# A decoder layer on one core: sixty-four bytes more behind each of the four tiles that hold split weights

## The chip, the cores and the metric

The kernel runs on one NeuronCore of a Trainium2 chip. The metric is device time of one execution, in microseconds, smaller is better. Several executions are timed and the median is given; beside them one execution is recorded instruction by instruction with the hardware profiler, and that record is what is called the profile or the trace here.

A NeuronCore has five instruction streams that run at the same time and wait for one another through semaphores: TensorE (PE, matrix products, with a separate row PEld in the profile for loading the stationary operand), VectorE (DVE), ScalarE (ACT), GpSimd (POOL) and SyncE (SP, which issues the DMA transfers here). Their common working memory is SBUF, 128 partitions side by side; an address below is a byte offset within a partition, the same in all 128.

## The reference, cut to what matters

One decoder layer: three token mixers on one normalised input, gated and merged, then a gated MLP with a short causal convolution. All in float32, 1024 positions, width 1024.

```python
h = _rmsnorm(x, g_mix[l])
(sb_q, sb_k, sb_v, ml_q, ml_k, ml_v, ml_o, ml_i, ml_f, xa_q, gate_pre) = jnp.split(
    h @ w_in[l], offsets, axis=-1)
...
merged = (gates[:, :, 0] * (y_sb @ w_sb_out[l])
          + gates[:, :, 1] * (y_ml @ w_ml_out[l])
          + gates[:, :, 2] * (y_xa @ w_xa_out[l]))
x = x + merged @ w_o[l]

h = _rmsnorm(x, g_ffn[l])
u = _causal_dwconv(h @ w_up[l], ff_conv_w[l], ff_conv_b[l])
u_val, u_gate = jnp.split(u, 2, axis=-1)
x = x + (jax.nn.silu(u_gate) * u_val) @ w_down[l]
```

Most of the arithmetic is in the dense products: the input projection, the three output projections with `w_o`, and the MLP.

## The kernel before, in words

**Split operands.** Each dense product is made in a faster number format (fp32r) from two parts per operand: `split` (L136, L137) writes a high part with ScalarE and the remainder, source minus high part, with VectorE. A product of two split operands is then three matmuls into one accumulator, in `mm3`: high by high (L149), high by low (L150), low by high (L151). Each of them streams 512 columns of one operand (the moving one) past a 128 x 128 block of the other (the stationary one, loaded ahead by PEld). The names in the profile's rows stand in the order output<-moving,stationary.

**Tiles in SBUF.** `T(shape, tag)` takes a tile from a pool; each tag has a ring of a fixed number of buffers, and the pool puts the rings one behind the other in SBUF. A page (`pg`, 16 buffers), `h` (16), `y` (2), `raw` (2), `whi` (2) and `wlo` (2) are all 4096 bytes per partition: 1024 numbers of 4 bytes. `whi` and `wlo` hold the split weights in three ways:

- `wsplit` (L139) takes one `whi` for the high parts and one `wlo` for the low parts of a 1024-number weight block. The matmuls of a product then load their stationary blocks in the order whi, whi, wlo. The projections of the first stage, the branch outputs and `w_o` are made so; `product` in the MLP's last stage splits into the same two tags.
- `qring` (L661), for the products in which `seven` computes a 2 x 2 block product with seven half-sized ones, takes one tile for both parts of half a weight block, by turns from `whi` and `wlo`. All twelve matmuls of such a product load from that one tile. The gates, the mLSTM and cross-attention columns of the input projection and the whole of the MLP's first product are made so.
- `mem_w` (L200) loads raw weights of the memory tokens' keys and values by turns into `raw`, `whi` and `wlo`, in the first 30 us.

In `nat_chunks` the roles are exchanged: the activations are stationary and `whi` and `wlo` are streamed. Half-sized tiles, `hf` (4 buffers of 2048 bytes), take the last, half-sized weight block and activation of each of the seven products of the MLP's last stage: twelve matmuls with both operands in `hf`.

**Where the tiles begin.** The built program places the rings as in this table, which gives the first byte of each buffer and its remainder by 256.

| tag | first bytes | remainder by 256 |
|---|---|---|
| `hf` | 19712, then every 2048 | 0 |
| `pg` | 28608, then every 4096 | 192 |
| `h` | 94144, then every 4096 | 192 |
| `y`, `raw` | 159680, 163776, 167872, 171968 | 192 |
| `whi` | 176064, 180160 | 192, 192 |
| `wlo` | 184256, 188352 | 192, 192 |
| `U` (5 buffers of 4096 or 4104 bytes) | 192448, then every 4128 | 192, 224, 0, 32, 64 |
| `me`, then `mw` or `px` | 213088, 217184 | 96 |

So before the change, apart from `hf`, every operand of the split products begins at the same remainder, and offsets inside a tile are multiples of 512 bytes.

**Order.** Each engine runs its instructions in the order in which the code (with a scheduler's priorities) recorded them; the rings' sizes decide how far a split can run ahead of the matmuls that read it.

Of the kernel before, what the change touches and what calls it, by code (L numbers as in the profile page):

```python
# [18 lines left out]
P = 128  # L19
D = 1024  # L20
S = 1024
# [21 lines left out]
def tile_hybrid_layer(ctx: ExitStack, tc: tile.TileContext, xT, memT, vecs, w_t, w_n, w_kv, w_if,  # L43
# [16 lines left out]
    def nm(s):  # L60
        uid[0] += 1
        return f"{s}_{uid[0]}"

    BUFS = {"h": 16, "pg": 16, "U": 5, "y": 2, "raw": 2, "whi": 2, "wlo": 2, "hf": 4, "me": 2,
            "mw": 4, "sm": 22, "px": 2}
    late = [None]

    def T(shape, tag, dt=F32, bufs=None):
        pool = {"mw": mlp, "mst": mlp, "px": late[0]}.get(tag, sb)
        return pool.tile(shape, dt, tag=tag, name=nm(tag), bufs=bufs or BUFS[tag])  # L70

    def page(tag="pg", dt=F32):
        return T([P, S], tag, dt)

    def half(dt=F32):
        return T([P, HALF], "hf", dt)

    def wide():
        return T([P, S], "U")
# [9 lines left out]
    def bank(tag):  # L89
        if tag in ("pj", "pv"):  # L90
            return ps.tile([P, HALF], F32, tag=tag, name=nm("ps_" + tag), bufs=2)
        if px1 is not None:
            if not spare.get(tag):
                t = two(tag)
                spare[tag] = [t[:, 1], t[:, 0]]
            return spare[tag].pop()
        return psx[0].tile([P, HALF], F32, tag=tag, name=nm("ps_" + tag), bufs=2)
# [4 lines left out]
    def hs(h):  # L102
        return slice(h * HALF, (h + 1) * HALF)
# [166 lines left out]
    def x_stats(xp):  # L270
        acc = []
        for i in range(4):
            sq = wide()
            nc.scalar.activation(sq, xp[i], AF.Square)
            acc.append(sq)
            if i:
                nc.vector.tensor_add(acc[0], acc[0], sq)
        a = acc[0][:, hs(0)]
        nc.vector.tensor_add(a, a, acc[0][:, hs(1)])
        return a  # L280
# [212 lines left out]
    a = x_stats(xp[0])  # L493
# [538 lines left out]
    for i in range(3 * KT):  # L1032
        b, n = i // KT, i % KT
# [5 lines left out]
        for h in (1, 0):  # L1039
            p = bank("pj")  # L1040
# [3 lines left out]
            dst, t = merged[n][:, hs(h)], th[:, hs(h)]  # L1044
# [360 lines left out]
```

## Time and profile before

| | |
|---|---|
| three timed executions | 1683.66, 1684.94, 1685.43 us |
| median | 1684.94 us |
| the profiled execution's own time | 1682.28 us |
| its span, first to last instruction | 1680.5 us |
| outside the span | 1.8 us |
| TensorE's mean granted clock | 0.999 of full |
| busy shares: DVE, ACT, POOL | 71%, 49%, 3% |

The profile's groups of instructions give for each line, engine and pair of tiles a count, the busy time in us, the mean duration of one in ns and the idle time of the engine just before. The duration of a matmul runs from its start to its modelled end, and matmuls overlap in the array, so 0.39 us in a row is not what one costs: the cost of a matmul in a dense stretch is the distance from its start to the next one's start, and that is read from the timeline, which prints start and duration of each. The view of busy times by stretch can be limited to the instructions that touch one tile, and then counts them.

### The profile page before, as it was taken

To read this page: it belongs to the slowest core of one execution; us is meant where nothing else is said; L and a number is where in the kernel's file an instruction comes from. 1 tells how busy PE (TensorE), PEld (TensorE's weight loads), DVE (VectorE), ACT (ScalarE), POOL (GpSimd) and SP (SyncE) were. 2 spreads that over 40 slices of the span, in tenths; PEclk is the share of its full clock that TensorE was granted. 3 is DMA by queue.
4 is the path that set the end of the run, shared out by engine and by line. 5 is a ranking of instruction groups with operands and counts; after the bars stand their busy time and mean duration, and the time that the engine had idled before them with its cause. 6 is when DMAs were issued, how large, how long until landed. Compare 5 with 4: busy or idle time off the path is not lost.

```text
span 1680.5 us, 21066 instructions
## 1 busy us (share of the span) xinstructions
PE 1652.2 (98%) x7927; PEld 1337.1 (80%) x7927; DVE 1193.2 (71%) x1682; ACT 819.1 (49%) x1237; POOL 51.8 (3%) x95
## 2 busy tenths in 40 slices
PE   8999999999999999999999999999999999999999
PEld 4777777787777888777788887688888888788887
DVE  5648777777954766555457648998777887789864
ACT  4547677645544445555312334565555555543431
POOL 1000000010000101000000000000000000000000
PEclk9999999999999999999999999999999999999999
DMA  8421011233334565322755354222222221486141
GB/s 295 147 64 33 26 39 51 98 122 114 124 115 151 189 188 169 133 100 82 264 196 191 112 178 167 82 95 90 99 76 76 75 86 66 163 326 238 33 140 72
DMA packets 96248, 212.68 MB, mean 127 GB/s; under 512 B 12416, under 2 KB 36224, under 8 KB 96148
## 3 DMA queue, kind: packets, MB, share of 16 engines
q1 hardware_dynamic: 96148, 211.35, 36.8%
q8 instruction: 62, 1.02, 0.3%
q14 instruction: 38, 0.31, 0.1%
HBM read 156.71 MB, written 54.61 MB: 126 GB/s over the span
## 4 chain that ended last, share of the span: by engine, by line
PE 90%; DVE 4%; ACT 4%; DMA 1%; issue 1%; SPq 0%; POOLq 0%; ACTq 0%; DVEq 0%
PE ps_pj L150 14%; PE ps_pj L149 14%; PE ps_pj L151 14%; PE ps_pv L151 6%; PE ps_pv L149 6%; PE ps_pv L150 6%; PE ps_tr L149 4%; PE ps_tr L151 4%; PE ps_tr L150 4%; PE ps_z L151 2%; PE ps_z L150 2%; PE ps_z L149 2%; PE ps_tr L434 2%; PE ps_pv L448 1%; PE ps_z L226 1%; PE ps_z L1005 1%
## 5 line engine op out<-in xcount | busy, mean ns | idle before, releaser
L150 PE MATMUL ps_pj<-h,whi 128*128 128x512 f32 x620 | 243.3, 392 | 0.0
L136 ACT ACTIVATE whi<-raw 128x512 fp32r<-128x512 f32 (+1 forms) x112 | 93.6, 835 | 185.7 <-PE ps_pj L150 81.4
L149 PE MATMUL ps_pj<-h,whi 128*128 128x512 f32 x412 | 163.7, 397 | 0.0
L149 PE MATMUL ps_pj<-pg,whi 128*128 128x512 f32 x396 | 155.1, 392 | 0.5 <-ACT U L699 0.5
L151 PE MATMUL ps_pj<-pg,wlo 128*128 128x512 f32 x380 | 148.1, 390 | 0.1
L150 PEld LDWEIGHTS ps_pj<-h,whi 128*128 128x128 f32 x620 | 116.5, 188 | 24.4 <-issue 1.0
L151 PE MATMUL ps_pj<-h,wlo 128*128 128x512 f32 x332 | 130.8, 394 | 0.5 <-DVE wlo L137 0.4
L810 DVE SCALAR_TENSOR_TENSOR y<-U,vec,y 128x1023 f32<-128x1023 f32 x88 | 112.4, 1279 | 7.5 <-ACT y L808 7.5
L422 DVE TENSOR_TENSOR_SCAN U<-U 128x512 f32<-128x512 f32 (+3 forms) x96 | 88.5, 964 | 30.7 <-ACT U L415 29.8
L149 PEld LDWEIGHTS ps_pj<-h,whi 128*128 128x128 f32 x412 | 77.4, 188 | 17.1 <-issue 0.9
L137 DVE TENSOR_TENSOR wlo<-raw,whi 128x1024 fp32r<-128x1024 f32 x54 | 66.0, 1222 | 32.0 <-ACT whi L136 32.0
L149 PEld LDWEIGHTS ps_pj<-pg,whi 128*128 128x128 f32 x396 | 74.5, 188 | 16.8 <-ACT U L699 0.9
L151 PEld LDWEIGHTS ps_pj<-pg,wlo 128*128 128x128 f32 x380 | 71.3, 188 | 15.6 <-DVE wlo L137 0.6
L136 ACT ACTIVATE whi<-pg 128x512 fp32r<-128x512 f32 (+1 forms) x59 | 43.4, 737 | 74.8 <-PE ps_pv L150 20.5
L150 PE MATMUL ps_pj<-pg,whi 128*128 128x512 f32 x188 | 74.8, 398 | 0.0
L151 PEld LDWEIGHTS ps_pj<-h,wlo 128*128 128x128 f32 x332 | 62.3, 188 | 14.7 <-DVE wlo L137 1.4
L150 PE MATMUL ps_pv<-h,whi 128*128 128x512 f32 x164 | 63.8, 389 | 0.0
L137 DVE TENSOR_TENSOR whi<-raw,whi 128x512 fp32r<-128x512 f32 x58 | 39.9, 688 | 32.2 <-ACT whi L136 32.1
L808 ACT ACTIVATE y<-U,vec 128x1024 f32<-128x1024 f32 x44 | 54.6, 1241 | 14.8 <-DVE U L712 14.7
L151 PE MATMUL ps_pj<-h,whi 128*128 128x512 f32 x156 | 60.8, 390 | 0.0
L151 PE MATMUL ps_tr<-pg,wlo 128*128 128x512 f32 x144 | 56.0, 389 | 0.0
L436 ACT ACTIVATE y<-ps_tr 128x1024 f32<-128x1024 f32 (+3 forms) x48 | 39.1, 814 | 31.6 <-PE ps_tr L434 31.2
(427 smaller groups left out, 4258.8 us busy)
## 6 DMA issues: line engine op xcount, KB each, us to landing
raw<-in_w_t_dram SPq DMA_DIRECT2D x29, 512.0 KB, 4.2
gate_d<-U SPq DMA_DIRECT2D x24, 512.0 KB, 3.2
U<-gate_d SPq DMA_DIRECT2D x24, 512.0 KB, 4.0
pg<-in_w_up_dram SPq DMA_DIRECT2D x22, 512.0 KB, 3.6
act_d<-y SPq DMA_DIRECT2D x22, 512.0 KB
pg<-in_w_t_dram SPq DMA_DIRECT2D x21, 512.0 KB, 3.9
raw<-in_w_dn_dram SPq DMA_DIRECT2D x18, 512.0 KB, 3.4
raw<-in_w_o_dram SPq DMA_DIRECT2D x16, 512.0 KB, 3.8
```

Of the source, the lines that this page charges most:

```text
L136: nc.scalar.activation(hi, src, AF.Copy)
L137: (eng or nc.vector).tensor_sub(lo, src, hi.bitcast(F32))
L149: nc.tensor.matmul(out, lh, rh, start=start, stop=False, skip_group_check=more)
L150: nc.tensor.matmul(out, lh, rl, start=False, stop=False, skip_group_check=more)
L151: nc.tensor.matmul(out, ll, rh, start=False, stop=stop, skip_group_check=more)
L226: nc.tensor.matmul(pm[m], mg[k // 4][:, c], w[:, hs(kk)], start=(k == 0), stop=(k == KT - 1))
L422: nc.vector.tensor_tensor_scan(f[:, a, 1:w + 1], f[:, a, 1:w + 1], f[:, a, 1:w + 1], 1.0 if o == 0 else f[:, a, 0:1], op0=ALU.mult, op1=AL ...
L434: nc.tensor.transpose(pt[:, a, ts(j)], g[:, a, ts(j)], ident)
L436: nc.scalar.activation(wt[:, :, :w], pt[:, :, :w], AF.Copy)
L448: nc.tensor.matmul(pv[64 * a:64 * a + 64, ts(rb % 4)], sbv[s // 2][:, s % 2, (2 * p + a) * 64:(2 * p + a + 1) * 64], wt[:, a, ts(j)], star ...
L808: nc.scalar.activation(out, u, AF.Identity, bias=bias, scale=taps[0])
L810: nc.vector.scalar_tensor_tensor(out[:, :S - s], u[:, s:], taps[s], out[:, :S - s], op0=ALU.mult, op1=ALU.add)
```

## The change

`T` gives tiles of the tags `whi` and `wlo` 16 numbers (64 bytes) more per partition than are used, and hands out the first 1024 numbers, shaped as before. Nothing is read from or written to the 64 bytes behind them.

```diff
     def T(shape, tag, dt=F32, bufs=None):
         pool = {"mw": mlp, "mst": mlp, "px": late[0]}.get(tag, sb)
+        if tag in ("whi", "wlo"):
+
+            t = pool.tile([P, S + 16], dt, tag=tag, name=nm(tag), bufs=BUFS[tag])[:, :S]
+            return t if len(shape) == 2 else t.rearrange("p (a b) -> p a b", a=shape[1])
         return pool.tile(shape, dt, tag=tag, name=nm(tag), bufs=bufs or BUFS[tag])
```

The instructions of the built program, their order on each of the five engines and their waits are the same, row for row, before and after; what differs is the addresses. The tiles that move are these:

| tag | first bytes after | later than before by | remainder by 256 after |
|---|---|---|---|
| `whi` | 176064, 180224 | 0, 64 | 192, 0 |
| `wlo` | 184384, 188544 | 128, 192 | 64, 128 |
| `U` | 192704, then every 4128 | 256 | 192, 224, 0, 32, 64, as before |
| `me`, `mw`, `px`, `mst` | 213344 and behind | 256 | as before |

The tensors in the chip's main memory stay where they were.

## The prediction

> **What bounds the kernel now.** I read the busy times and the granted clock first, then the chain that ended last, then what TensorE waited for, then the timeline of TensorE in a dense stretch.
>
> ```profile
> span 1680.5 us, 21066 instructions
> PE 1652.2 (98%) x7927; PEld 1337.1 (80%) x7927; DVE 1193.2 (71%) x1682; ACT 819.1 (49%) x1237; POOL 51.8 (3%) x95
> PEclk9999999999999999999999999999999999999999
> PE 90%; DVE 4%; ACT 4%; DMA 1%; issue 1%; SPq 0%; POOLq 0%; ACTq 0%; DVEq 0%
> PE ps_z L226 <- DMA raw<-in_w_kv_dram: 6.3, 1, 6.3
> PE ps_tr L434 <- DVE U L424: 3.7, 5, 1.6
> ```
>
> TensorE is busy for 98% of the span, at full clock, and makes 90% of the chain. Its two longest waits are 6.3 us for the first weights and 3.7 us in five pieces. So only the pace of the matmuls can move the time by much. That pace, far from any restart, is this (the matmuls in between, of the same three lines, are left out):
>
> ```profile
> 999.65 0.39 PE L149 MATMUL ps_pj<-pg,whi 128*128 128x512 f32 x1
> 999.88 0.39 PE L150 MATMUL ps_pj<-h,whi 128*128 128x512 f32 x1
> 1000.11 0.39 PE L151 MATMUL ps_pj<-pg,wlo 128*128 128x512 f32 x1
> ...
> 1003.50 0.39 PE L151 MATMUL ps_pj<-pg,wlo 128*128 128x512 f32 x1
> ```
>
> From 999.65 to 1003.50 there are 17 steps: 3.85 / 17 = 0.2265 us each. Here pages, `whi` and `wlo` all begin at remainder 192 by 256, and the loads and streams inside them are shifted against each other by multiples of 512 bytes.
>
> How many matmuls does the change touch? The view of busy times limited to one tile counts those that read `whi` (first row) and `wlo` (second row):
>
> ```profile
> 0.00:1681.00 1681.00, 941.26 (x3372) 630.46 (x3372) 194.99 (x224) 173.63 (x224) 1.00 0.37 127
> 0.00:1681.00 1681.00, 749.73 (x2572) 481.64 (x2572) 195.01 (x224) 92.12 (x147) 1.00 0.37 127
> ```
>
> The first two counts are PE and PEld: 3,372 + 2,572 = 5,944 matmuls, three quarters of all 7,927. Each ns on the step of one is 5.9 us of the end. About 0.2% of the time (3.4 us) is what a measurement of this kernel can tell from no change; that is 0.57 ns a matmul.
>
> **The change, part by part.** It adds and removes no instruction, wait or transfer, and moves none past another: the count of each is unchanged, and the sum of those terms is 0. What can change is how long an instruction takes at its new address.
>
> *VectorE and ScalarE.* The trace already has splits between tiles that begin at different remainders: sources `raw` and `pg` at 192 like the target, `hf` at 0, `px` and `me` at 96.
>
> ```profile
> L137 DVE TENSOR_TENSOR whi<-raw,whi 128x512 fp32r<-128x512 f32 x58 | 39.9, 688 | 32.2 <-ACT whi L136 32.1
> L137 DVE TENSOR_TENSOR whi<-hf,whi 128x512 fp32r<-128x512 f32 x21 | 14.5, 691 | 19.8 <-ACT whi L136 19.6
> L137 DVE TENSOR_TENSOR whi<-me,whi 128x512 fp32r<-128x512 f32 x8 | 5.5, 686 | 3.2 <-ACT whi L136 3.2
> L136 ACT ACTIVATE whi<-raw 128x512 fp32r<-128x512 f32 x58 | 36.3, 626 | 34.2 <-PE ps_pv L151 22.3 <-issue 6.1 <-PE ps_tr L151 2.1
> L136 ACT ACTIVATE whi<-hf 128x512 fp32r<-128x512 f32 x21 | 13.1, 624 | 2.4 <-PE ps_pv L151 2.4
> L136 ACT ACTIVATE whi<-me 128x512 fp32r<-128x512 f32 x8 | 5.0, 629 | 3.8 <-PE ps_pv L151 2.5 <-PE ps_z L151 1.3
> ```
>
> Means of 688, 691 and 686 ns on VectorE and 626, 624 and 629 on ScalarE: 5 ns apart at most. For the 448 VectorE instructions on the two tiles that bounds the cost at 2.2 us either way, and it lies under TensorE's 98%; with that cover gone it would still be below what can be told. I take 0. `U`, `me`, `mw` and `px` move by 256 bytes and keep their remainders; I take 0 for them too, with the same 2.2 us as bound.
>
> *Loads into the moved tiles.* The 6.3 us wait at the start ends with a transfer into `raw`, which isn't moved. 0.
>
> *The weight load.* It now starts at remainders 192, 0, 64 or 128. The trace has loads from other remainders: transposes that load from `U` (192, 224, 0, 32, 64), `pg` (192) and `hf` (0), and products whose weights lie in `hf`.
>
> ```profile
> L434 PEld LDWEIGHTS ps_tr<-ident,U 128*128 128x128 f32 x288 | 31.9, 140 | 13.2 <-issue 7.9 <-ACT y L436 2.8 <-ACT pg L136 0.8
> L916 PEld LDWEIGHTS ps_tr<-ident,pg 128*128 128x128 f32 x32 | 4.0, 139 | 1.0
> L247 PEld LDWEIGHTS ps_tr<-ident,hf 128*128 128x128 f32 x8 | 1.0, 140 | 0.3
> L149 PEld LDWEIGHTS ps_pj<-h,whi 128*128 128x128 f32 x412 | 77.4, 188 | 17.1 <-issue 0.9 <-DVE U L1048 0.8 <-ACT h L136 0.2
> L149 PEld LDWEIGHTS ps_pj<-hf,hf 128*128 128x128 f32 x8 | 1.5, 188 | 0.3
> ```
>
> 139 to 140 ns for transposes and 188 for products, wherever the block begins. The load itself costs nothing more or less.
>
> *The pace of load and stream together.* This is the one term that the trace doesn't settle: nowhere does a long run of split products have stationary and moving operand at different remainders. The nearest rows are the twelve matmuls with both operands in `hf`, at remainder 0, after pages at 192:
>
> ```profile
> 1673.62 0.39 PE L151 MATMUL ps_pj<-pg,wlo 128*128 128x512 f32 x1
> 1673.84 0.39 PE L149 MATMUL ps_tr<-hf,hf 128*128 128x512 f32 x1
> ...
> 1674.07 0.39 PE L150 MATMUL ps_tr<-hf,hf 128*128 128x512 f32 x1
> ...
> 1674.73 0.69 DVE L1229 TENSOR_TENSOR U<-U,ps_tr 128x512 f32<-128x512 f32 x1 [9.42 <-PE ps_tr L151]
> ...
> 1676.38 0.39 PE L151 MATMUL ps_pj<-hf,hf 128*128 128x512 f32 x1
> ```
>
> While the matmul at 1673.62 streams from a page, the first block of `hf` is loaded: exactly the mixed case. Its step is 0.22 us, to the last digit that the row has the dense pace. But the eleven steps within `hf` take 2.54 us, 0.2309 each: 4.4 ns over the dense pace, although both operands have equal remainders again. Two readings are possible. Either a jump between remainders disturbs the pace for some ten matmuls, or the end of a product does (VectorE's evictions start in the same stretch, at 1674.73). Upper end: 4.4 ns on all 5,944, 26.2 us. Lower end: the nearest wide matmuls with a shorter regular step, the scores of the cross-attention, plain float32 with 256 columns, where a matmul is two records.
>
> ```profile
> 669.84 1.73 PE ps_z L980 x8
> ```
>
> 1.73 / 8 = 0.2163 us a record, 10.2 ns under the dense pace; on 5,944 that is 60.6 us. So the term lies between -60.6 and +26.2 us. I take the row nearest to the mixed case, the step at 1673.62, and that is 0.
>
> On the pace the Trainium skill, "TensorE: Matmul & The Clock Gate", section "Wait — 56ns, not 53.3ns?", gives 215.7 ns from start to start with 512 columns at full clock; by it the split products would have 10.8 ns to lose, and an estimate from that page is 64 us for 5,944. The trace's 226.5 ns disagrees with the page's figure, in another number format. On whether the address can free it, "SBUF — State Buffer", section "Who interferes with whom", says that TensorE has two separate read ports, for the stream and for the weight load, and waits for no one: by that rule the sum is 0. No row here shows ports; the 0.22 us step of the mixed case agrees with it.
>
> **Sum.** 0 (instructions) + 0 (splits) + 0 (transfers) + 0 (weight load) + 0 (pace) = 0, against the profiled execution's 1682.28 us, of which 1680.5 are span and 1.8 lie around it. That execution lies 2.7 us under the median of the three timed ones, so the median to expect is theirs, 1684.9 us.
>
> **Rivals.**
>
> *Slower: the jump disturbs.* The mechanism is the first reading above. Before, the remainder jumps into and out of `hf` only seven times each. After, each product of `seven` loads from the next of four tiles, so the distance between stationary and moving operand changes every twelve matmuls, and with `wsplit` it changes twice in every three (whi, whi, wlo). If each jump of the stationary operand costs what the passage into `hf` costs, nearly all 5,944 run at 0.2309: +26 us, 1711. If only the products of `seven` settle again or the disturbance is smaller, a third of that: +9, 1694. It decides from 0.57 ns a matmul on. For it: eleven slow steps that no wait explains. Against it: in `hf` the moving operand jumps too, and the pages that are streamed past `whi` and `wlo` don't move here; and the one step in which only the stationary block had jumped was not slow.
>
> *Faster: equal remainders are the reason for the slow pace.* If the stream and the weight load meet in the same part of SBUF because all tiles begin alike, and that is what separates 0.2265 from 0.2163, shifts of 64 to 192 bytes free part or all: three quarters of the loads are shifted, so up to 0.75 x 60.6 = 45 us, 1640; with a tenth of it 4.5 us, 1680. For it: the gap is there, in nearly every step. Against it: the step with mixed remainders should have been shorter and isn't, and shifts by any multiple of 512 bytes, of which the dense stretch has many, all give the same pace.
>
> *It doesn't do what it says.* A pool could round the longer tiles up so that all remainders stay alike; the addresses in the built program exclude it, so this gets no chance.
>
> **How the numbers follow.** No change: 0.62. The jump disturbs, or some other cost of the mixed remainders: 0.23. Shorter steps: 0.15. The unchanged case holds its own range of 1682 to 1688 (the executions before lie between 1683.66 and 1685.43). Of the slower case's 0.23 I put 0.16 below 1702 (two thirds of the full price), of the faster one's 0.15 about 0.06 above 1677, since there a small gain is less likely than the whole. 1677 to 1702 then leaves out 0.07 above and 0.09 below. The ends that the bounds allow, 1640 and 1711, lie outside.
>
> **What would show it.** One group of those that read `whi` stands for the others:
>
> ```profile
> L150 PE MATMUL ps_pj<-h,whi 128*128 128x512 f32 x620 | 243.3, 392 | 0.0
> ```
>
> Right, if in the changed kernel's timeline a dense stretch of L149, L150 and L151 still has steps of 0.2265 us whichever of the four tiles the weights lie in; if that group stays at 392 ns; and if L136 and L137 keep 624 to 629 and 686 to 691 ns. The slower rival would show as steps of 0.23 and matmuls of 0.40 us scattered through products of `seven`, the faster one as steps towards 0.22. The forecast would be wrong if the steps depend on which tile holds the weights; the twelve matmuls of one product against those of the next tell that at once.

## The result, and the profile after

The changed kernel takes 1703.79 us (median of four, 1703.12 to 1706.60) against 1684.30 us for the kernel before (median of four): ratio 1.0121, 95% interval 1.0109 to 1.0133. It is slower by 1.2%, outside the range of the prediction. Its span in the profile is 1702.0 us, 21.5 us more than before. The line numbers are four higher than before: L149 to L151 are now L153 to L155.

The page's busy times and granted clock, and TensorE's longest waits, of the changed kernel:

```profile
span 1702.0 us, 21066 instructions
PE 1674.5 (98%) x7927; PEld 1339.3 (79%) x7927; DVE 1194.9 (70%) x1682; ACT 819.2 (48%) x1237; POOL 52.4 (3%) x95
PEclk9999999999999999999999999999999999999999
PE ps_z L230 <- DMA raw<-in_w_kv_dram: 6.2, 1, 6.2
PE ps_tr L438 <- DVE U L428: 3.6, 5, 1.6
```

TensorE's busy time has grown by 22.3 us, VectorE's by 1.7 and ScalarE's by 0.1. TensorE's carries the whole difference; the clock is full, and the longest waits are within 0.1 us of what they were. The same matmuls, as many as before, follow one another more slowly. The groups that the prediction named, of the changed kernel:

```profile
L154 PE MATMUL ps_pj<-h,whi 128*128 128x512 f32 x620 | 245.3, 396 | 0.0
L153 PEld LDWEIGHTS ps_pj<-h,whi 128*128 128x128 f32 x412 | 77.6, 188 | 18.1 <-DVE U L1052 1.0 <-issue 0.9 <-ACT h L140 0.2
L141 DVE TENSOR_TENSOR whi<-hf,whi 128x512 fp32r<-128x512 f32 x21 | 14.5, 692 | 20.6 <-ACT whi L140 20.4
L140 ACT ACTIVATE whi<-hf 128x512 fp32r<-128x512 f32 x21 | 13.1, 624 | 2.5 <-PE ps_pv L155 2.5
```

Loads (188 ns) and splits (692 and 624 ns) are as before. The matmul group has gone from 392 to 396 ns. The timeline shows where. These are the first matmuls of five products of `seven` in a row; the eleven others of each are left out:

```profile
466.34 0.39 PE L153 MATMUL ps_pj<-pg,whi 128*128 128x512 f32 x1
...
469.09 0.40 PE L153 MATMUL ps_pj<-h,wlo 128*128 128x512 f32 x1
...
471.88 0.39 PE L153 MATMUL ps_pv<-h,whi 128*128 128x512 f32 x1
...
474.68 0.40 PE L153 MATMUL ps_pj<-h,wlo 128*128 128x512 f32 x1
...
477.48 0.39 PE L153 MATMUL ps_pv<-pg,whi 128*128 128x512 f32 x1
```

Twelve steps take 2.75 us in the first product and 2.79, 2.80 and 2.80 in the next three, which is 0.2292 a step against 0.2325 to 0.2333; before, every one had 0.2265. By the program's addresses their weights lie 0, 128, 64 and 192 bytes from the streamed pages, by remainder. So the pace depends on the tile that holds the weights, which is what the prediction had named as the sign that it was wrong. Even the first product, at 0 as before the change, is slower than it was then; what came just before it counts too, as the run history below shows. In what follows, *distance* is the start of the stationary block minus the start of the streamed one, by remainder of 256.

### The profile page after: what moved, and what is told of

Same layout as the page of the kernel before. It is cut to its first block, busy times and chain, and to the rows that moved or that the text cites. A ratio compares the mean times of both kernels' runs of the same rounds, so it can differ in the third digit from the quotient of the medians.

```text
span 1702.0 us, 21066 instructions
## 1 busy us (share of the span) xinstructions
PE 1674.5 (98%) x7927; PEld 1339.3 (79%) x7927; DVE 1194.9 (70%) x1682; ACT 819.2 (48%) x1237; POOL 52.4 (3%) x95
## 4 chain that ended last, share of the span: by engine, by line
PE 90%; ACT 4%; DVE 4%; DMA 2%; issue 1%; POOL 0%; POOLq 0%; SPq 0%; ACTq 0%; DVEq 0%
PE ps_pj L153 14%; PE ps_pj L154 14%; PE ps_pj L155 14%; PE ps_pv L154 6%; PE ps_pv L155 6%; PE ps_pv L153 6%; PE ps_tr L153 4%; PE ps_tr L154 4%; PE ps_tr L155 4%; PE ps_z L155 2%; PE ps_z L154 2%; PE ps_z L153 2%; PE ps_tr L438 1%; PE ps_pv L452 1%; PE ps_z L230 1%; PE ps_z L1009 1%
## 5 line engine op out<-in xcount | busy, mean ns | idle before, releaser
L153 PE MATMUL ps_pj<-h,whi 128*128 128x512 f32 x412 | 165.2, 401 | 0.5 <-DVE U L1052 0.5
L153 PE MATMUL ps_pj<-pg,whi 128*128 128x512 f32 x396 | 157.1, 397 | 0.7 <-ACT U L703 0.4
L155 PE MATMUL ps_pj<-pg,wlo 128*128 128x512 f32 x380 | 150.0, 395 | 0.1
L155 PE MATMUL ps_pj<-h,wlo 128*128 128x512 f32 x332 | 131.9, 397 | 0.5 <-DVE wlo L141 0.4
L153 PEld LDWEIGHTS ps_pj<-h,whi 128*128 128x128 f32 x412 | 77.6, 188 | 18.1 <-DVE U L1052 1.0
L153 PEld LDWEIGHTS ps_pj<-pg,whi 128*128 128x128 f32 x396 | 74.6, 188 | 19.4 <-ACT U L703 1.3
L155 PEld LDWEIGHTS ps_pj<-pg,wlo 128*128 128x128 f32 x380 | 71.5, 188 | 17.4 <-DVE wlo L141 0.6
L140 ACT ACTIVATE whi<-pg 128x512 fp32r<-128x512 f32 (+1 forms) x59 | 43.4, 737 | 80.5 <-PE ps_pv L154 21.5
L155 PEld LDWEIGHTS ps_pj<-h,wlo 128*128 128x128 f32 x332 | 62.5, 188 | 15.9 <-DVE wlo L141 1.4
L141 DVE TENSOR_TENSOR whi<-raw,whi 128x512 fp32r<-128x512 f32 x58 | 39.9, 688 | 33.2 <-ACT whi L140 33.0
L155 PE MATMUL ps_pj<-h,whi 128*128 128x512 f32 x156 | 61.4, 394 | 0.0
L155 PE MATMUL ps_tr<-pg,wlo 128*128 128x512 f32 x144 | 56.9, 395 | 0.0
L141 DVE TENSOR_TENSOR wlo<-raw,wlo 128x512 fp32r<-128x512 f32 x58 | 39.9, 688 | 22.6 <-ACT wlo L140 22.4
```

The costliest lines, as they stand in the source:

```text
L140: nc.scalar.activation(hi, src, AF.Copy)
L141: (eng or nc.vector).tensor_sub(lo, src, hi.bitcast(F32))
L153: nc.tensor.matmul(out, lh, rh, start=start, stop=False, skip_group_check=more)
L155: nc.tensor.matmul(out, ll, rh, start=False, stop=stop, skip_group_check=more)
```

## The experiments

Three theories stood against one another. **A**: the standing distance sets the pace. **B**: only a change of the distance disturbs, for some ten matmuls (the prediction's slower rival). **C**: the remainder of the stationary block alone counts.

### The distance by itself: scan

A kernel with nothing but bursts of 32 fp32r matmuls, 512 columns, TensorE alone. Names give the bytes: m192w64 streams from remainder 192 and loads from 64.

```diff
+PLAN = [(192, w) for w in range(0, 512, 16)] + [(m, w) for m in (0, 64, 128) for w in range(0, 512, 64)]
+    for n, (m, w) in enumerate(PLAN):
+        p = ps.tile([P, HALF], F32, tag="z", name=f"m{m}w{w}z", bufs=2)
+        for i in range(BURST):
+            a = m // 4 + HALF * (i % 2)
+            b = w // 4 + P * (i % 4)
+            nc.tensor.matmul(p, wts[:, b:b + P], mov[:, a:a + HALF], start=(i == 0), stop=(i == BURST - 1))
```

> Leaves the whole layer out: only split-format matmuls (128x512, 32 in a row into one bank) from two tiles, TensorE alone, the stationary block beginning w bytes and the stream m bytes behind a multiple of 512; m192 with w from 0 to 496 in steps of 16, then m 0, 64, 128 with w in steps of 64. Theory A (the standing distance between stream and weight load sets the pace): groups with w = m run at 0.2267 us a matmul, w = m + 64 near 0.2333, m + 128 near 0.232, m + 192 near 0.229, the same in all 32, whatever m is. Theory B (only a change of the distance disturbs, for about ten matmuls): every group starts with steps near 0.231 and then runs at 0.2267, a mean of 0.228, whatever w is. Theory C (the remainder of the stationary block alone counts, 192 good): w = 192 is quick for every m.

The timeline of the scan merges each burst into a row. The distance from one row's start to the next one's, by 32, is the pace:

```profile
83.32 7.63 PE L70 MATMUL m192w160z<-mov,wts 128*128 128x512 f32 x32
90.78 7.43 PE L70 MATMUL m192w176z<-mov,wts 128*128 128x512 f32 x32
98.06 7.42 PE L70 MATMUL m192w192z<-mov,wts 128*128 128x512 f32 x32
105.31 7.42 PE L70 MATMUL m192w208z<-mov,wts 128*128 128x512 f32 x32
112.57 7.62 PE L70 MATMUL m192w224z<-mov,wts 128*128 128x512 f32 x32
120.03 7.63 PE L70 MATMUL m192w240z<-mov,wts 128*128 128x512 f32 x32
...
246.21 7.45 PE L70 MATMUL m0w0z<-mov,wts 128*128 128x512 f32 x32
253.50 7.63 PE L70 MATMUL m0w64z<-mov,wts 128*128 128x512 f32 x32
260.97 7.60 PE L70 MATMUL m0w128z<-mov,wts 128*128 128x512 f32 x32
268.41 7.49 PE L70 MATMUL m0w192z<-mov,wts 128*128 128x512 f32 x32
275.74 7.43 PE L70 MATMUL m0w256z<-mov,wts 128*128 128x512 f32 x32
283.01 7.63 PE L70 MATMUL m0w320z<-mov,wts 128*128 128x512 f32 x32
```

At equal remainders, 98.06 to 105.31 is 7.25 / 32 = 0.2266 us. With the stream at 0, distance 64 gives 0.2334, 128 gives 0.2325, 192 gives 0.2291, and 256 is quick again. B would have a mean of 0.228 in every burst, and the slow bursts have 0.2325 to 0.2334, so B doesn't describe them. C falls too: m0w0 loads from remainder 0 and is quick (0.2278, with the first steps of the burst, which still settle), and m0w192 loads from 192 and has 0.2291. At a stream of 192 the bursts 16 bytes either side (w176, w208) are quick too. One thing didn't fit A: with the stream at 192, the burst at 128, distance 192, took 0.2334 and not 0.229. No burst was quicker than those at equal remainders. The rows are one execution.

### The distance in the layer: shift64, all64, pad256

Unused bytes move whole rings, either all four weight buffers alike (shift64) or the pages with them (all64). In pad256 the change's own padding is four times as long.

```diff
# shift64, against the kernel before; all64 has "pg" in place of "whi"
+        if tag == "whi" and not spaced:
+            spaced.append(sb.tile([P, 16], F32, tag="gap", name="gap"))
+            nc.gpsimd.memset(spaced[0], 0.0)
# pad256, against the changed kernel
-            t = pool.tile([P, S + 16], dt, tag=tag, name=nm(tag), bufs=BUFS[tag])[:, :S]
+            t = pool.tile([P, S + 64], dt, tag=tag, name=nm(tag), bufs=BUFS[tag])[:, :S]
```

> The kernel before with 64 unused bytes once ahead of the first whi buffer, so all four buffers begin 64 bytes later than the pages by remainder, and keep one distance among themselves. Theory A: all 5,944 run at the pace that products with that distance have in the changed kernel, 0.2333 against 0.2267: +39 us, 1723. Theory B: the distance changes as seldom as before, so 1685. Theory C: as A, 1723.

> The kernel before with 64 unused bytes ahead of the pages, so that pages, h, y, raw, whi and wlo all begin at remainder 0 like hf. Theory A: 1684, since all distances are multiples of 512, and the slow steps at hf are gone (0.4 us). Theory B: 1684. Theory C: 1723, since every stationary block begins at remainder 0.

> The changed kernel with 256 bytes in place of 64 behind each of the four tiles: they begin 0, 256, 512 and 768 bytes later, all remainders by 256 as before. If the distance counts by 256 or less (A, C with period 256): 1684. If it counts by 512 (A with period 512): half of the products are at distance 256, and the time lies between 1690 and 1705. Theory B, if a jump by 256 is a jump: 1700.

| | median | ratio to before (95% interval) |
|---|---|---|
| shift64 | 1716.65 us | 1.0193 (1.0177 to 1.0208) |
| all64 | 1684.08 us | 0.9996 (0.9986 to 1.0005) |
| pad256 | 1683.66 us | 1.0000 (0.9990 to 1.0009) |

The kernel before had 1684.46 us beside them. shift64 keeps one standing distance and is slower than the change itself: B gives 1685 for it and falls as the main cause. all64 loads from remainder 0 and is not slow: C falls again. pad256 jumps by 256 bytes as often as the change jumps by 64, and costs nothing: 256 bytes are a full turn. The first matmuls of two products in shift64, and the first and last of the twelve `hf` matmuls in all64:

```profile
1300.03 0.40 PE L153 MATMUL ps_pv<-h,whi 128*128 128x512 f32 x1
...
1302.83 0.40 PE L153 MATMUL ps_tr<-h,wlo 128*128 128x512 f32 x1
```

```profile
1676.36 0.39 PE L153 MATMUL ps_tr<-hf,hf 128*128 128x512 f32 x1
...
1678.85 0.39 PE L155 MATMUL ps_pj<-hf,hf 128*128 128x512 f32 x1
```

In shift64 2.80 / 12 = 0.2333 us, as in the scan at 64. Its 32 us are less than the 39 expected. In the profiles TensorE's busy time is 34.4 us longer than before (1686.6 against 1652.2) and the span 33.2 us (1713.7 against 1680.5), so waits that are now covered make about 1 us of the gap. The 5,944 also count some matmuls in plain float32 and some that stream `whi` or `wlo`; how much that makes was not worked out. In all64 the eleven steps take 2.49 us, 0.2264 each, where the kernel before had 0.2309: with pages and `hf` at one remainder the slow passage is gone. That was the row from which the prediction took its upper end.

### How near is near enough: late16 and late32

```diff
# late16, against the changed kernel; late32 has 8 in place of 4
-            t = pool.tile([P, S + 16], dt, tag=tag, name=nm(tag), bufs=BUFS[tag])[:, :S]
+            t = pool.tile([P, S + 64], dt, tag=tag, name=nm(tag), bufs=BUFS[tag])[:, 4:S + 4]
```

> The changed kernel with the four tiles each beginning 16 bytes later than a page by remainder (256 bytes longer, used from byte 16 on). The scan had 0.2267 us a matmul at distances of 16 either way. Theory A with that window: 1684, within 0.2% of the kernel before. If in the full kernel any unequal remainder is slow: 1717, as in shift64.

> As late16, but 32 bytes later. The scan had 0.2334 us a matmul at a distance of 32 (w224 beside m192), 6.7 ns over the quick pace. Theory A with the scan's window: as shift64, whose 5,944 matmuls ran 6.6 ns slower: 1717, between 1713 and 1720. If the window were wider in the full kernel: 1684.

late32 came out as expected, 1715.81 us, ratio 1.0192 (1.0175 to 1.0209). late16 fits neither expectation: 1705.43 us, ratio 1.0133 (1.0098 to 1.0169), and its four executions scatter from 1699.32 to 1713.04, where those of every other version of the layer lie within 5.3 us. Its timeline, two products at the same distance 16 in one execution:

```profile
466.96 0.39 PE L153 MATMUL ps_pj<-pg,whi 128*128 128x512 f32 x1
...
469.76 0.39 PE L153 MATMUL ps_pj<-h,wlo 128*128 128x512 f32 x1
```

```profile
1300.02 0.39 PE L153 MATMUL ps_pj<-pg,whi 128*128 128x512 f32 x1
...
1302.74 0.39 PE L153 MATMUL ps_z<-h,wlo 128*128 128x512 f32 x1
```

2.80 us for twelve steps in the first, 0.2333 each, and 2.72 in the second, 0.2267. One distance, two paces. So theory A lacked something, and a new one was needed.

### What came before: history

Theory **H**: at some distances two repeating patterns of steps exist, and the state in which a burst begins picks one. Pairs of bursts, the first at one distance and the second at another; d16p64then is distance 16 after 64.

```diff
+PLAN = [x for d in (16, 192, 240, 128, 32, 0) for p in (0, 64, 32, 128) for x in ((p, f'd{d}p{p}first'), (d, f'd{d}p{p}then'))]
```

> Leaves the whole layer out: TensorE alone, fp32r, 512 columns, stream at remainder 0. Pairs of bursts of 32: first at distance 0, 64, 32 or 128, then at the distance d asked for (16, 192, 240, 128, 32, 0). Theory H (a distance can have two standing patterns, and what came before picks one; this is why the layer at distance 16 scattered from 1699 to 1713): d16 after 0 runs at 0.2267 us a matmul, d16 after 64 or 32 near 0.233; d192 near 0.229 after one and 0.233 after another. Theory N (the distance alone decides, and the slow stretches of the layer at 16 come from other engines' work): d16 runs at 0.2267 after every predecessor, and each d has one pace. Both: d0 returns to 0.2267 within ten matmuls.

```profile
15.88 7.42 PE L70 MATMUL d16p0then<-mov,wts 128*128 128x512 f32 x32
...
30.61 7.63 PE L70 MATMUL d16p64then<-mov,wts 128*128 128x512 f32 x32
...
60.44 7.42 PE L70 MATMUL d16p128then<-mov,wts 128*128 128x512 f32 x32
...
74.95 7.49 PE L70 MATMUL d192p0then<-mov,wts 128*128 128x512 f32 x32
...
89.74 7.63 PE L70 MATMUL d192p64then<-mov,wts 128*128 128x512 f32 x32
...
326.44 7.45 PE L70 MATMUL d0p64then<-mov,wts 128*128 128x512 f32 x32
```

Here the second number, first start to last end, is compared: 7.42 us is a burst at about 0.2267 a step, 7.63 one at about 0.2334. Distance 16 is quick after 0 and after 128 and slow after 64 and 32 (7.63 both), with no other engine at work. Distance 192 is 7.49 after 0 and 7.63 after 64, so the burst of the scan that hadn't fitted has the second of two paces (there it came after distance 176). Distance 240 took 7.42 after 0 and 7.47 or 7.48 after the others; 32 and 128 were slow after every predecessor (7.59 to 7.62). Distance 0 comes back to the quick pattern after every predecessor tried. H holds and N falls. It fits the scatter of late16: which pattern a stretch falls into depends on its beginning, and chance delays could throw it from one into the other (this last step was not tried by itself).

The changed kernel shows the same in the layer. In the products of the MLP's first stage the four tiles come in another order than in the five products of the result, where it was 0, 128, 64, 192:

```profile
1142.39 0.39 PE L153 MATMUL ps_pv<-pg,whi 128*128 128x512 f32 x1
...
1145.12 0.39 PE L153 MATMUL ps_tr<-h,wlo 128*128 128x512 f32 x1
...
1147.87 0.40 PE L153 MATMUL ps_pj<-pg,whi 128*128 128x512 f32 x1
...
1150.66 0.39 PE L153 MATMUL ps_z<-h,wlo 128*128 128x512 f32 x1
...
1153.46 0.39 PE L153 MATMUL ps_tr<-pg,whi 128*128 128x512 f32 x1
```

The twelve steps have 0.2275, 0.2292, 0.2325 and 0.2333 us each. Going by the paces, and by the turns that the buffers take, the distances are 0, 192, 64 and 128: here 192 comes after 0 and has 0.2292, where there it came after 64 and had 0.2333, and 0 comes after 128 and has 0.2275, where there it came after 192 and had 0.2292.

### One part of the change alone: wlo128

```diff
# against the kernel before
+        if tag == "wlo" and not spaced:
+            spaced.append(sb.tile([P, 32], F32, tag="gap", name="gap"))
+            nc.gpsimd.memset(spaced[0], 0.0)
```

> One part of the change alone: 128 unused bytes once ahead of the first wlo buffer, so whi keeps distance 0 and both wlo buffers stand at 128. 2,572 matmuls use wlo. If only the standing distance costs: 2,572 x 5.8 ns (0.2325 against 0.2267) = 15 us, less some 3 us of waits that a slower TensorE swallows, as in the changed kernel: 1696. If each return from 128 to 0 costs as well (the steps 0.229, 0.232, 0.231 that follow it in the changed kernel, and no settling at all in whi, whi, wlo triads): 5 to 7 us more, 1701 to 1703.

1705.26 us against 1683.17: ratio 1.0133 (1.0116 to 1.0150), 22 us. The standing distance alone accounts for 15 us before covered waits. So the changes between 128 and 0 cost as well, and somewhat more than expected. In `wsplit` products, where whi, whi, wlo alternate between 0 and 128, the first two rows from the timeline of wlo128 show it:

```profile
1009.76 0.40 PE L155 MATMUL ps_pj<-pg,wlo 128*128 128x512 f32 x1
...
1012.53 0.40 PE L155 MATMUL ps_pj<-pg,wlo 128*128 128x512 f32 x1
...
1303.96 0.40 PE L153 MATMUL ps_pj<-pg,whi 128*128 128x512 f32 x1
...
1306.71 0.40 PE L153 MATMUL ps_z<-h,wlo 128*128 128x512 f32 x1
```

Twelve steps in 2.77 us, 0.2308 each. Standing distances alone, two at 0.2267 and one at 0.2325, would give 0.2286. The last two rows are a product of `seven` at distance 0 after one at 128: 2.75 us for twelve steps, 0.2292. B is thus a part of the cost, beside A. A return from 128 does not always cost: in history the burst at 0 after 128 took 7.42 us, as after 0. What decides between the two was not found.

### Which matmuls: kinds

> Leaves the whole layer out: bursts of 32 matmuls at distances 0, 64, 128 and 192 for fp32r with 512 columns (r512), the same with one unchanging stationary block (s512), with 384, 256 and 128 columns, plain float32 with 512 and 128 columns and bfloat16 with 512 and 128. Theory A1 (stream and weight load hinder each other whenever the load runs beside a stream at one column a cycle): r512, s512, r384 and r256 are all slower at 64 and 128 than at 0, by 3 to 7 ns a matmul, and plain float32 with 512 columns, whose step of 0.429 us leaves the load ample time, is the same at all four. Theory A2 (the step only depends on the distance where it is about as long as load plus start, 0.224 to 0.236): r512 and s512 vary, r384, r256 and r128 do not. bfloat16 is open: no row so far has it.

```diff
+PLAN = [(k, w) for k in ('r512', 's512', 'r384', 'r256', 'r128', 'f512', 'f128', 'b512', 'b128') for w in (0, 64, 128, 192)]
+            nc.tensor.matmul(p[:, :n], wts[k[0]][:, b:b + P], mov[k[0]][:, a:a + n], start=(i == 0), stop=(i == BURST - 1))
```

```profile
71.48 5.74 PE L75 MATMUL r384w0z<-movr,wtsr 128*128 128x384 f32 x32
77.06 5.81 PE L75 MATMUL r384w64z<-movr,wtsr 128*128 128x384 f32 x32
...
88.34 5.71 PE L75 MATMUL r384w192z<-movr,wtsr 128*128 128x384 f32 x32
93.89 4.00 PE L75 MATMUL r256w0z<-movr,wtsr 128*128 128x256 f32 x32
97.72 3.94 PE L75 MATMUL r256w64z<-movr,wtsr 128*128 128x256 f32 x32
...
150.82 27.63 PE L75 MATMUL f512w64z<-movf,wtsf 128*128 128x512 f32 x64
178.29 27.63 PE L75 MATMUL f512w128z<-movf,wtsf 128*128 128x512 f32 x64
...
261.81 7.07 PE L75 MATMUL b512w0z<-movb,wtsb 128*128 128x512 bf16 x31
268.71 7.07 PE L75 MATMUL b512w64z<-movb,wtsb 128*128 128x512 bf16 x31
```

r512 and s512 behave alike at 64, 128 and 192: whether the load brings new weights or the same ones makes no difference (r512 at 0, 9.03 us, is the run's first burst and holds its slow start). With 384 columns the distance counts too: 0.1744 at 0 (71.48 to 77.06), 0.1766 at 64 and 0.1734 at 192, so 0 is better than 64 and no better than 192. With 256 columns 0 is worse than 64, 0.1197 against 0.1181. With 128 columns 64, 128 and 192 all have 0.1116. Plain float32 and bfloat16 are the same at every distance, float32 at 27.47 / 64 = 0.4292 a record (a matmul is two) and bfloat16 at 6.90 / 32 = 0.2156 (its x31 is a record that the trace lacks). Neither A1 nor A2 holds: A1 had 256 columns wrong, A2 both 384 and 256. What is shown is that of the three formats only fp32r has the effect, and that its sign between 0 and 64 depends on the length of the stream. Each burst was run once and with one predecessor, so the paces with fewer columns may have a second pattern that this run doesn't show.

## Why the prediction was wrong, point by point

- **The bound** was right: TensorE at 98% before and after, and its busy time grew by 22.3 us and the span by 21.5, the 0.8 us between them being idle time of TensorE that has gone.
- **Instructions, splits, transfers, weight load** at 0 were right: 692 and 624 ns against 691 and 624, 188 ns against 188, the first wait 6.2 us against 6.3.
- **The pace of load and stream together** is the step that failed: "I take the row nearest to the mixed case, the step at 1673.62, and that is 0." The runs showed 2.5 to 6.8 ns more a matmul in its place, at standing distances of 64 to 192, and 22.3 us in all. One step cannot show a pattern that repeats over several: in the recorded starts of the scan's burst m0w192 the steps run 229, 232, 226 ns over and over, so one in three is quick by itself; and a step carries the state that the ones before it left. The right reading of the same rows was the other one: eleven steps of 0.2309 that nothing but a change of remainders explained. all64 showed that they were that.
- **The upper end**, 4.4 ns on 5,944 matmuls, 26.2 us, was of the right size by luck. Within `hf` both operands begin at 0, so its 4.4 ns is what settling again costs, and, as the prediction says, no long run of split products in the trace before stands at another distance than 0. By the scan's paces a matmul costs 6.8 ns more at distance 64, 5.9 at 128 and 2.5 at 192. `whi` stands at 0 and 64, `wlo` at 128 and 192, each for half its matmuls: 1,686 x 6.8 + 1,286 x (5.9 + 2.5) = 22 us, against 22.3 of added busy time. That this comes so near is partly luck too. On average the sum adds 3.8 ns a matmul; the first four products shown in the section on the result have 0.2321, 5.4 ns over 0.2267, since 192 is at its slower pace there and 0 has to settle, and the four of the MLP's first stage have 0.2306, 3.9 ns over it.
- **The slower rival** had the sign, with 0.23. Its mechanism, the jump, is a part (some 7 of the 22 us in wlo128, with 15 reckoned for the standing distance). The larger part, the standing distance, which alone cost 32 us in shift64, falls under the "other cost of the mixed remainders" of the chances, without a price. Its argument against itself, that the streamed pages don't move, was no argument, since only the difference matters.
- **The faster rival** fell: no distance is quicker than 0 with 512 columns. The 0.2163 from which it took its price is a float32 record with 256 columns; with 512 columns a float32 record takes 0.4292 us (kinds), so the gap between 0.2265 and 0.2163 was no sign that anything was held up.
- The rule of the Trainium skill that gave 0 ("SBUF — State Buffer", section "Who interferes with whom": two separate read ports, TensorE waits for no one) doesn't cover these rows: with TensorE alone at work, the same matmuls take 0.2266 or 0.2334 us by their addresses. The measurement decides. The figure of the Trainium skill's page "TensorE: Matmul & The Clock Gate", section "Wait — 56ns, not 53.3ns?", 215.7 ns from start to start, agrees with bfloat16 here (0.2156) and not with fp32r.

No version beats the kernel before: all64, which also removes the slow passage at `hf`, is the same within 0.1%. What in the hardware makes the distance count, and why by 256 bytes, stays open.

## What to carry to other kernels

For dense fp32r products with 512 columns, let the tiles that are streamed and the tiles that are loaded as weights begin at the same remainder by 256 bytes; 64 bytes behind each of the four weight tiles cost 1.2% here, and a shift of all four by 64 or by 32 bytes against the pages 1.9%. A ring whose buffers are whole multiples of 256 bytes keeps this by itself, and a small tile put in front of it can lose it. When a trace has one passage with steps that no wait explains, look at the whole passage before taking a single step from it as the price.

## What the runs showed of the hardware that was not expected

- In these runs the pace of fp32r matmuls with 512 columns is one of several repeating patterns: 0.2267 us at distance 0, 0.2325 to 0.2334 at 64 and 128, 0.2291 or 0.2334 at 192.
- At distances 16 and 192 two patterns exist and the preceding distance picks one (from first start to last end 7.42 or 7.63 us, and 7.49 or 7.63 us, for 32 matmuls).
- With 256 columns distance 0 is the slower one, 0.1197 against 0.1181 us; with 512 columns float32 (27.46 to 27.52 us for 64 records) and bfloat16 (6.90 or 6.91 for 32) don't depend on it.
